# Four operand splits and one softmax scaling moved between engines in the attention stage of a hybrid trunk kernel

## The chip, the cores and the metric

The kernel runs on one NeuronCore of a Trainium2 chip, in one launch. The metric is the device time of that launch in microseconds. The kernel before took 1543.39 us (median of three runs, 1543.29 to 1546.81). The engines are called as the profile calls them: PE (matrix products and transposes), DVE (VectorE), ACT (ScalarE), POOL (GpSimd) and SP (the queue that issues most DMAs). Each engine works through its instructions in order.

## The reference

One layer over 1024 frames of width 1024, in 32-bit floats. The parts that matter here, cut short:

```python
def band_attention(q, k, v, qn_g, kn_g, rel_bias):      # 8 heads of 64, chunks of 64 frames
    qh = head_rms(q, qn_g); kh = head_rms(k, kn_g)
    scores = einsum('bnqhd,bnkhd->bnhqk', qc, kb) * 64 ** -0.5   # own chunk and the 8 before
    scores = where(valid, scores + bias, -1e30)
    probs = softmax(scores, axis=-1)
    o = einsum('bnhqk,bnkhd->bnqhd', probs, vb)

h = rmsnorm(x, norm_mix_g)
oa = hgrn2_mixer(...)                                   # 4 heads of 128, a gated recurrence
ob = band_attention(...)
merged = sigmoid(gate_a) * (oa @ w_branch_a) + sigmoid(gate_b) * (ob @ w_branch_b)
x = x + merged @ w_out
x = x + (silu(h2 @ w_gate) * (h2 @ w_up)) @ w_down      # h2 = rmsnorm(x)
x = x + sigmoid(h3 @ w_ple_gate) * (p @ w_ple_proj)     # h3 = rmsnorm(x)
```

## The kernel before

**Split operands.** A large product keeps nearly full precision by taking each operand as two: `hi` is the value rounded to the PE's fast type (a cast, on ACT), `lo` is the remainder, value minus `hi` (a subtraction). Three products, hi·hi, hi·lo and lo·hi, are summed in PSUM (`gemm`). Weights come as 128x1024 pieces: a load into `wr`, a cast to `wh` on ACT (L142) and a remainder `wl`, in the attention stage on GpSimd (L149, L150). Activations lie in `s` tiles ("slots").

**Stages.** The projections and norms come first, then the four heads of the recurrence, woven with projections for the attention; then the attention itself; then `branches`, which multiplies `oa` and `ob` with the branch weights; then the output product, the feed-forward part and the last gate. Between the recurrence and the branches the four tiles of `oa` lie in DRAM.

**The attention stage** (`attention`, L721) runs 32 steps. Step n takes a pair of heads and a block of 128 queries: steps 0 to 15 take the blocks of pairs 0 and 1 in turn, steps 16 to 31 those of pairs 2 and 3. Work of neighbouring steps overlaps. Step n, in the order that the code records it:

- head 1 of step n-1 gets its reciprocal and scaling (`stage(n - 1, 1)`);
- a piece of other PE work (`next(feed)`): up to step 27 the projections of the later pairs of queries and keys, from step 29 on the branches;
- the scores of step n, and on DVE the sum with the bias and the running extreme, straight from PSUM (a custom operation);
- in odd steps the products of probabilities and values for steps n-3 and n-2;
- `stack(n + 1)`: two transposes of the next queries and keys, two ACT copies out of PSUM that round them, and two DVE remainders; then another piece of feed;
- the transposes of head 1 of step n-1 (`pt(n - 1, 1)`), the exponentials of both heads of step n on ACT, the transposes of head 0 of step n-1 (`pt(n - 1, 0)`), then head 0's reciprocal on DVE and scaling.

The profile names head 0's scores `m` and head 1's `s`; their transposes are `pm<-eye,m` and `pm<-eye,s` at L105. A step with all five blocks in its band has 128x640 scores per head; the first blocks of a pair have 128, 256, 384 and 512.

**What sets the order.** Operations called through `self.V`, `self.A`, `self.G`, `self.load`, `self.mul` and `self.tr` are pinned: each engine executes them in the order in which the Python code calls them (the helper at L72, for DMAs L97, for matmuls L102, for transposes L105). Operations called on the engine directly, the weight casts of L142 among them, are placed by the scheduler. GpSimd's instructions in this stage are all pinned: powers for the norms of queries and keys (`m<-m,mhalf`, in odd steps), the weight remainders `wl` and the issues of accumulating DMAs (`next(self.adds)`, odd steps, and in `branches`).

**The branch operands.** `branch_load` loads the four `oa` tiles back (`raws`), and at the end of four steps, listed in `SPLITS`, one of them is split: a pinned ACT cast and a pinned DVE remainder. The pairs are read by the branch products, the first of them in step 29 (the first two) and step 30 (the last two).

Of the kernel before, what the change touches and what calls it, by code (L numbers as in the profile page):

```python
# [11 lines left out]
F32R = mybir.dt.float32r  # L12
U8 = mybir.dt.uint8
U32 = mybir.dt.uint32
AF = mybir.ActivationFunctionType
ALU = mybir.AluOpType
# [6 lines left out]
HALF = 512  # L23
NFF = 22
STEPS = (NFF // 2 + 1) // 2
SPLITS = (24, 26, 27, 28)
EPS = 1e-6
LEVELS = (1, 2, 4, 8, 16)
TURN = 32
# [15 lines left out]
def f32(ap):  # L45
    return ap.bitcast(F32)
# [28 lines left out]
class Trunk:  # L75
# [585 lines left out]
    def attn_scores(self, pair, b):  # L661

        nb = min(b + 1, 5)
        cols = nb * P
        k0 = (b + 1 - nb) * P
        na = {1: 1, 2: 2, 3: 3, 4: 2, 5: 3}[nb] * P
        q1, q2 = self.qs.pop((pair, b))
        k1, k2 = self.ks[pair % 2]
        parts = [(lo, hi) for lo, hi in ((0, na), (na, cols)) if hi > lo]
        banks = [[self.mm() for _ in parts] for _ in range(2)]  # L670
        for i, (lo, hi) in enumerate(parts):
            c = slice(k0 + lo, k0 + hi)
            for j, (q, k) in enumerate(((q1, k1), (q1, k2), (q2, k1))):
                for h in range(2):
                    r = slice(64 * h, 64 * h + 64)
                    self.mul(banks[h][i][:, :hi - lo], q[r, :], k[r, c], start=j == 0, stop=j == 2)

        def softmax(h):
            bias = self.bias[pair, h]
            s = self.slot(late=True)[:, :640] if h else self.small(640, tag="s")  # L680
            mx = self.small(2, tag="mx2")
            last = None
            for i, (lo, hi) in enumerate(parts):
                init = 3.0e38 if last is None else last
                self.V.tensor_tensor_reduce(
                    s[:, lo:hi], banks[h][i][:, :hi - lo], bias[:, 640 - cols + lo:640 - cols + hi], -1.0, init, ALU.add, ALU.min, mx[:, i:i + 1])
                last = mx[:, i:i + 1]
            yield s, nb
            den = self.small(1, tag="den")
            self.A.activation(s[:, :cols], s[:, :cols], AF.Exp, bias=last, scale=-1.0, accum_out=den)  # L690
            yield
            self.V.reciprocal(den, den)
            if h == 0:
                self.A.activation(s[:, :cols], s[:, :cols], AF.Copy, scale=den)
            else:
                self.V.tensor_scalar(s[:, :cols], s[:, :cols], den, None, ALU.mult)

        return [softmax(h) for h in range(2)]

    def attn_pt(self, s, nb):  # L700
# [20 lines left out]
    def attention(self):  # L721

        steps = [(2 * two + p, b) for two in range(2) for b in range(8) for p in range(2)]
        whole = len(steps)
        feed = self.feed
        sc, pts = {}, {}

        def stack(n):
            if n >= whole:
                return iter(())  # L730
            p, b = steps[n]
            if b == 0:
                for h in range(2):
                    bt = self.small(640, tag="bias")
                    self.load(bt, self.d["bias"][2 * p + h])
                    self.bias[p, h] = bt
            return self.attn_stack(p, b)

        def scores(n):
            for h, stages in enumerate(self.attn_scores(*steps[n])):  # L740
                sc[n, h] = (*next(stages), stages)

        def stage(n, h):
            if 0 <= n < whole:
                next(sc[n, h][2], None)

        def pt(n, h):
            if 0 <= n < whole:
                pts[n, h] = self.attn_pt(*sc[n, h][:2])

        def pv(n):
            if 0 <= n < whole:
                self.attn_pv(*steps[n], (pts.pop((n, 0)), pts.pop((n, 1))), sc[n, 0][1])

        for i in range(FIRST, 8):
            next(feed, None)
            if i == FIRST:
                self.hgrn_gate()
            if i == 7:
                drain(stack(0))  # L760
                drain(self.hgrn_out())
        drain(self.copies)
        self.adds = chain(self.osum, self.wsum)
        for n in range(whole + 2):
            if n % 2 and n < whole:
                next(self.adds)
            stage(n - 1, 1)
            next(feed, None)
            if n < whole:
                if steps[n][1] == 0:  # L770
                    self.ob.append(self.slot())
                scores(n)
            if n % 2:
                pv(n - 3)
                pv(n - 2)
            drain(stack(n + 1))
            if n < whole - 3 or n >= whole:
                next(feed, None)
            pt(n - 1, 1)
            stage(n, 0)  # L780
            stage(n, 1)
            pt(n - 1, 0)
            stage(n, 0)
            self.rest(False)
            if n > whole - 5:
                self.rest(False)
            if n == 0:
                self.keep_heads(self.oa, self.od, self.done_heads)
            if n == whole // 2 + 3:
                self.keep_heads(self.ob, self.obd, [0, 1])  # L790
            if n == whole - 10:
                raws = self.branch_load(self.od)
            if n in SPLITS:
                raw = raws[len(self.osrc)]
                hi, lo = self.slot(F32R), self.slot(F32R)
                self.A.copy(hi, raw)
                self.V.tensor_tensor(lo, raw, f32(hi[:, :]), ALU.subtract)
                self.osrc.append((hi, lo))
            if n == whole - 4:
                while self.queue:  # L800
                    self.rest()
                self.queue = None
                self.gate_load()
                self.gate_load()
                self.branch = self.branches()
                feed = chain(feed, self.branch)
            yield 0
        self.keep_heads(self.ob, self.obd, [2, 3])
# [1283 lines left out]
def drain(stream):  # L2092
    while True:
        try:
            next(stream)
        except StopIteration as e:
            return e.value
# [125 lines left out]
```

## Time and profile before

| | us |
|---|---|
| median of three runs | 1543.39 |
| the runs | 1546.81, 1543.29, 1543.39 |
| the profiled execution | 1546.48 |
| its span | 1544.7 |
| PE, DVE, ACT, GpSimd busy | 1517.0, 1107.8, 661.5, 634.2 |
| attention stage, about | 448 to 646 of the span |

A row of a timeline gives start and duration in us, engine, line of the code, operation, output and inputs by the program's names, partitions x elements, count, and in brackets the time that the engine sat idle before it and what ended that wait. A row of a windows table gives a stretch of the span, its length, then the busy time and count of instructions of PE, PE's weight loads, DVE, ACT and GpSimd, then the clock granted to the PE (1.00 is full speed), the DMA engines' share and GB/s. In tables of waits, "X <- Y: a, b, c" means that X waited for Y a us in total, in b waits, the longest c. The chain of waits is the work that ended last, followed back.

### The profile page before, as it was taken

To read this page: it belongs to the slowest core of one execution; us is meant where nothing else is said; L and a number is where in the kernel's file an instruction comes from. 1 tells how busy PE (TensorE), PEld (TensorE's weight loads), DVE (VectorE), ACT (ScalarE), POOL (GpSimd) and SP (SyncE) were. 2 spreads that over 40 slices of the span, in tenths; PEclk is the share of its full clock that TensorE was granted. 3 is DMA by queue.
4 is the path that set the end of the run, shared out by engine and by line. 5 is a ranking of instruction groups with operands and counts; after the bars stand their busy time and mean duration, and the time that the engine had idled before them with its cause. 6 is when DMAs were issued, how large, how long until landed. Compare 5 with 4: busy or idle time off the path is not lost.

```text
span 1544.7 us, 20689 instructions
## 1 busy us (share of the span) xinstructions
PE 1517.0 (98%) x7692; PEld 1252.4 (81%) x7692; DVE 1107.8 (72%) x1603; ACT 661.5 (43%) x1109; POOL 634.2 (41%) x353
## 2 busy tenths in 40 slices
PE   8999999999999998999999999999999999999998
PEld 6888888888877877788888888888888888888886
DVE  5777776577766767547888877777777757756678
ACT  6633333433346767522566222222222234456452
POOL 4233333101132423245212656665555545545546
PEclk9999999999999999999999999999999999999999
DMA  5552434698543365476346244443333288775335
GB/s 207 190 170 82 143 144 148 222 323 304 183 137 64 93 168 157 142 220 224 118 145 214 99 117 126 124 128 114 106 102 103 102 308 319 275 271 179 127 101 199
DMA packets 97908, 258.66 MB, mean 167 GB/s; under 512 B 10128, under 2 KB 14992, under 8 KB 97296
## 3 DMA queue, kind: packets, MB, share of 16 engines
q1 hardware_dynamic: 91264, 241.60, 44.8%
q0 software_dynamic: 6400, 15.73, 6.1%
q8 instruction: 60, 0.98, 0.2%
q14 instruction: 40, 0.33, 0.1%
q10 hardware_dynamic: 144, 0.02, 0.0%
HBM read 194.13 MB, written 94.63 MB: 187 GB/s over the span
## 4 chain that ended last, share of the span: by engine, by line
PE 91%; DVE 5%; DMA 1%; ACT 1%; issue 1%; SPq 0%; POOL 0%; DVEq 0%; ACTq 0%; POOLq 0%
PE pm L102 89%; DVE s L72 3%; PE pm L105 3%; DMA m<-d 0%; ACT wh L142 0%; DMA s<-in_x 0%; DVE m L72 0%; ACT s L72 0%; DMA wr<-in_fm 0%; ACT m L72 0%; DMA wr<-in_wv 0%; DVE s L337 0%; SPq L97 0%; DVE s L234 0%; DVE wl L72 0%
## 5 line engine op out<-in xcount | busy, mean ns | idle before, releaser
L102 PE MATMUL pm<-s,whi 128*128 128x512 f32 x1848 | 568.9, 389 | 0.0
L102 PE MATMUL pm<-s,wh 128*128 128x512 f32 (+1 forms) x1520 | 472.2, 392 | 6.8 <-ACT wh L142 5.2
L102 PEld LDWEIGHTS pm<-s,whi 128*128 128x128 f32 x1848 | 346.8, 188 | 72.0 <-DVE t L72 0.2
L102 PE MATMUL pm<-s,wlo 128*128 128x512 f32 x924 | 359.4, 389 | 0.0
L102 PEld LDWEIGHTS pm<-s,wh 128*128 128x128 f32 x1520 | 284.5, 189 | 66.6 <-ACT wh L142 5.2
L72 DVE TENSOR_TENSOR s<-s,s 128x512 f32<-128x512 f32 (+3 forms) x240 | 293.3, 1251 | 60.7 <-ACT s L72 47.0
L102 PE MATMUL pm<-s,wl 128*128 128x512 f32 (+1 forms) x760 | 296.4, 390 | 0.5 <-POOL wl L150 0.5
L150 POOL TENSOR_TENSOR wl<-wr,wh 128x1024 fp32r<-128x1024 f32 (+2 forms) x72 | 175.7, 2445 | 220.8 <-ACT wh L142 209.8
L72 DVE TENSOR_TENSOR t<-pm,t 128x512 f32<-128x512 f32 x163 | 112.2, 689 | 140.9 <-PE pm L102 118.4
L102 PEld LDWEIGHTS pm<-s,wlo 128*128 128x128 f32 x924 | 173.5, 188 | 36.0
L142 ACT CAST wh<-wr 128x1024 fp32r<-128x1024 f32 (+2 forms) x104 | 104.2, 1005 | 206.9 <-PE pm L102 90.0
L102 PE MATMUL pm<-wh,s 128*128 128x512 f32 x512 | 181.9, 409 | 0.0
L102 PEld LDWEIGHTS pm<-s,wl 128*128 128x128 f32 x760 | 143.3, 189 | 31.0 <-POOL wl L150 1.2
L72 POOL TENSOR_TENSOR wlo<-q,whi 128x512 fp32r<-128x512 f32 x64 | 102.6, 1604 | 151.9 <-ACT whi L72 81.6
L72 POOL TENSOR_TENSOR wlo<-wr,whi 128x1024 fp32r<-128x1024 f32 (+1 forms) x65 | 136.0, 2099 | 68.0 <-ACT whi L72 58.9
L72 POOL TENSOR_TENSOR m<-m,mhalf 128x8 f32<-128x8 f32 (+1 forms) x24 | 35.1, 1462 | 223.4 <-DVE m L72 223.4
L72 ACT CAST whi<-q 128x512 fp32r<-128x512 f32 (+1 forms) x96 | 72.8, 758 | 106.9 <-PE pm L102 87.1
L72 ACT CAST s<-s 128x1024 fp32r<-128x1024 f32 (+1 forms) x98 | 94.4, 982 | 55.2 <-DVE s L72 32.0
L102 PEld LDWEIGHTS pm<-wh,s 128*128 128x128 f32 x512 | 97.0, 189 | 18.9 <-DVE m L72 0.2
L72 POOL TENSOR_TENSOR s<-t,rb 128x512 f32<-128x512 f32 x44 | 71.2, 1619 | 99.4 <-ACT t L72 99.4
L102 PE MATMUL pm<-wl,s 128*128 128x512 f32 x256 | 100.5, 393 | 0.0
L72 ACT ACTIVATE t<-s 128x512 f32<-128x512 f32 x44 | 27.8, 633 | 158.6 <-DVE s L72 154.5
(151 smaller groups left out, 1758.5 us busy)
## 6 DMA issues: line engine op xcount, KB each, us to landing
s<-d SPq DMA_DIRECT2D x83, 512.0 KB, 6.2
d<-s SPq DMA_DIRECT2D x87, 256.0 KB, 2.3
wr<-d SPq DMA_DIRECT2D x36, 512.0 KB, 3.5
d<-s SPq DMA_DIRECT2D x32, 512.0 KB, 4.3
d<-t SPq DMA_DIRECT2D x50, 256.0 KB, 2.6
wr<-in_sz SPq DMA_DIRECT2D x22, 512.0 KB, 5.8
wr<-in_sg SPq DMA_DIRECT2D x22, 512.0 KB, 3.7
wr<-in_su SPq DMA_DIRECT2D x22, 512.0 KB, 4.1
```

Source lines behind the costliest of these rows:

```text
L72: return lambda *a, **k: self.trunk.order(op(*a, **k), self.key)
L102: return self.order(self.nc.tensor.matmul(*a, **k))
L105: return self.order(self.nc.tensor.transpose(*a, **k))
L142: self.nc.scalar.copy(hi[:, c], raw[:, c])
L150: rest.tensor_tensor(lo[:, c], raw[:, c], f32(hi[:, c]), ALU.subtract)
```

## The change

Three things change, all in the attention stage:

1. The scaling of head 0's probabilities, 32 instructions of up to 128x640, goes from ACT to GpSimd, pinned there. Head 1's stays on DVE.
2. Each of the four splits of branch operands moves from the end of a step to the place behind `stack(n + 1)`, in front of the second piece of feed, and its remainder goes from DVE to GpSimd. The steps are 23, 25, 27 and 28 in place of 24, 26, 27 and 28.
3. The loads of the four operands are recorded one step earlier (step 21 in place of 22).

```diff
-SPLITS = (24, 26, 27, 28)
+SPLITS = (23, 25, 27, 28)
...
             self.V.reciprocal(den, den)
-            if h == 0:
-                self.A.activation(s[:, :cols], s[:, :cols], AF.Copy, scale=den)
-            else:
-                self.V.tensor_scalar(s[:, :cols], s[:, :cols], den, None, ALU.mult)
+            (self.V if h else self.G).tensor_scalar(s[:, :cols], s[:, :cols], den, None, ALU.mult)
...
             drain(stack(n + 1))
+            if n in SPLITS:
+                raw = raws[len(self.osrc)]
+                hi, lo = self.slot(F32R), self.slot(F32R)
+                self.A.copy(hi, raw)
+                self.G.tensor_tensor(lo, raw, f32(hi[:, :]), ALU.subtract)
+                self.osrc.append((hi, lo))
             if n < whole - 3 or n >= whole:
                 next(feed, None)
...
-            if n == whole - 10:
+            if n == whole - 11:
                 raws = self.branch_load(self.od)
-            if n in SPLITS:
-                raw = raws[len(self.osrc)]
-                hi, lo = self.slot(F32R), self.slot(F32R)
-                self.A.copy(hi, raw)
-                self.V.tensor_tensor(lo, raw, f32(hi[:, :]), ALU.subtract)
-                self.osrc.append((hi, lo))
```

The order of GpSimd's instructions at the end of the stage, from step 27 on, as the difference of the two programs. `m_6143` and `m_6147` are the power of step 27; `s_6136` and `s_6214` remainders of branch operands; `m_6095`, `m_6197`, `m_6294`, `m_6386`, `m_6454` head 0 of steps 27 to 31; `wl` remainders of branch weights:

```order
-L72 TENSOR_TENSOR m_6143<-m_6143,mhalf 128x8
+L72 TENSOR_TENSOR s_6136<-s_5639,s_6135 128x1024
+L72 TENSOR_TENSOR m_6147<-m_6147,mhalf 128x8
+L72 TENSOR_SCALAR m_6095<-m_6095,m_6161 128x640
+L72 TENSOR_TENSOR s_6214<-s_5641,s_6213 128x1024
+L72 TENSOR_SCALAR m_6197<-m_6197,m_6227 128x640
 L72 DMA d_3019<-d_2971 128x1024
 L72 TENSOR_TENSOR wl_6254<-wr_6256,wh_6255 128x1024
 L72 TENSOR_TENSOR wl_6260<-wr_6262,wh_6261 128x1024
 L72 DMA d_3170<-d_3119 128x1024
+L72 TENSOR_SCALAR m_6294<-m_6294,m_6344 128x640
+L72 TENSOR_SCALAR m_6386<-m_6386,m_6412 128x640
```

The scaling of step 29 (`m_6294`) now stands behind the two weight remainders and a DMA issue; before, GpSimd had no softmax work at all.

ACT in step 29 and at the start of step 30, before: the exponentials of step 29 (`m_6294`, `s_6298`), head 0's scaling, two copies of the stack, two copies of transposes (`m_6348`, `m_6402`), and the casts of the two branch weights.

```order
L72 ACTIVATE m_6294,m_6344<-m_6294,m_6295 128x640
L72 ACTIVATE s_6298,m_6346<-s_6298,m_6299 128x640
L72 COPY m_6348<-pm_6349 128x384
L72 ACTIVATE m_6294<-m_6294,m_6344 128x640
L72 ACTIVATE s_3912<-pm_6394,cols 128x128
L72 ACTIVATE m_6397<-pm_6394,ones 128x128
L72 COPY m_6402<-pm_6403 128x384
L142 CAST wh_6255<-wr_6256 128x1024
L142 CAST wh_6261<-wr_6262 128x1024
```

And with the change:

```order
L72 ACTIVATE m_6294,m_6344<-m_6294,m_6295 128x640
L72 ACTIVATE s_6298,m_6346<-s_6298,m_6299 128x640
L72 COPY m_6348<-pm_6349 128x384
L142 CAST wh_6255<-wr_6256 128x1024
L72 ACTIVATE s_3912<-pm_6394,cols 128x128
L72 ACTIVATE m_6397<-pm_6394,ones 128x128
L142 CAST wh_6261<-wr_6262 128x1024
L72 COPY m_6402<-pm_6403 128x384
```

The scaling is gone, and the first cast stands where it stood; both casts are still behind the exponentials of step 29.

DVE at the end of step 27 and the start of step 28, before (copies of transposes out of PSUM, the reciprocals, the remainder `s_6174`, head 1's scaling, and a scaling of queries and keys):

```order
L72 COPY m_6147<-pm_6153 128x256
L72 COPY m_6161<-pm_6167 128x256
L72 RECIPROCAL m_6157<-m_6157 128x1
L72 TENSOR_TENSOR s_6174<-s_5706,s_6173 128x1024
L72 RECIPROCAL m_6159<-m_6159 128x1
L72 TENSOR_SCALAR s_6099<-s_6099,m_6159 128x640
L72 TENSOR_TENSOR m_6179<-pm_5981,m_6143 128x512
```

And with the change:

```order
L72 COPY m_6151<-pm_6157 128x256
L72 COPY m_6165<-pm_6171 128x256
L72 RECIPROCAL m_6161<-m_6161 128x1
L72 RECIPROCAL m_6163<-m_6163 128x1
L72 TENSOR_SCALAR s_6099<-s_6099,m_6163 128x640
L72 TENSOR_TENSOR m_6179<-pm_5985,m_6147 128x512
```

The remainder between the two reciprocals is gone; the rest keeps its order.

## The prediction

> **What bounds the kernel now.** I read the page's first part, then the PE's waits inside the attention stage, then the chain of waits, and only then single rows of the four engines.
>
> ```profile
> PE 1517.0 (98%) x7692; PEld 1252.4 (81%) x7692; DVE 1107.8 (72%) x1603; ACT 661.5 (43%) x1109; POOL 634.2 (41%) x353
> ...
> PE 91%; DVE 5%; DMA 1%; ACT 1%; issue 1%; SPq 0%; POOL 0%; DVEq 0%; ACTq 0%; POOLq 0%
> ```
>
> The matrix engine is busy for 98% of the span and carries 91% of the chain. Work taken off the other engines is worth something only where the PE waits for it. The change touches the attention stage alone, from about 448 to 646 us of the span. The PE's waits there, in us in total, times and longest, are these:
>
> ```profile
> PE pm L105 <- DVE s L72: 4.4, 2, 3.8
> PE pm L102 <- DVE m L72: 1.2, 1, 1.2
> PE pm L105 <- ACT m L72: 0.8, 2, 0.5
> PE pm L105 <- DVE m L72: 0.4, 1, 0.4
> ```
>
> That is 6.8 us in all, and 3.8 of it is one stall. The chain of waits shows what leads up to that stall (start, us, what):
>
> ```profile
> 611.08 0.83 DVE m L72 x3
> ...
> 611.93 0.83 ACT m L72
> 612.76 0.94 ACT s L72
> ...
> 613.73 1.23 DVE s L72
> ...
> 615.06 0.56 DVE s L72
> ...
> 615.76 2.37 PE pm L105 x10
> ```
>
> This is step 27 turning into step 28. DVE finishes copying transposes and takes head 0's reciprocal. ACT then scales head 0 (611.93) and makes the cast of a branch operand (612.76). DVE, in order, waits for that cast, does the 1.23 us remainder, and only then scales head 1 (615.06), for which the PE's transposes wait. So a cast and a remainder that nothing needs for another 2 us or more stand in front of work that the PE needs at once. The rows of the PE around it (start, us):
>
> ```profile
> 615.76 1.30 PE L105 MATMUL pm<-eye,s 128*128 128x128 f32 x5 [3.78 <-DVE s L72]
> 616.86 1.27 PE L105 MATMUL pm<-eye,m 128*128 128x128 f32 x5
> 617.78 1.12 PE L102 MATMUL pm<-s,wh 128*128 128x512 f32 x2
> ...
> 627.69 0.74 PE L105 MATMUL pm<-eye,s 128*128 128x128 f32 x5
> 628.94 0.77 PE L105 MATMUL pm<-eye,m 128*128 128x128 f32 x5 [0.51 <-ACT m L72]
> 629.47 0.70 PE L102 MATMUL pm<-s,wh 128*128 128x512 f32 x2
> ...
> 635.15 0.82 PE L105 MATMUL pm<-eye,s 128*128 128x128 f32 x5 [0.64 <-DVE s L72]
> 636.26 0.73 PE L105 MATMUL pm<-eye,m 128*128 128x128 f32 x5 [0.29 <-ACT m L72]
> ```
>
> After the stall the same three groups take 1.30, 1.27 and 1.12 us where they later take 0.74, 0.77 and 0.70: 1.5 us more. The granted clock (the third last column of the windows) says why:
>
> ```profile
> 616.00:618.00 2.00, 2.00 (x11) 2.00 (x11) 1.71 (x8) 1.12 (x2) 0.00 (x0) 0.50 0.71 137
> ```
>
> **The change, part by part.** *Loads one step earlier: 0.* The four loads stand at the same place of SP's queue in both programs, and SP is far ahead of the steps: they go out as the four `s<-d` here, some 30 us before the first cast.
>
> ```profile
> 552.61 2.41 SPq L97 DMA_DIRECT2D s<-d  x4
> ```
>
> *Remainders and casts.* Four remainders of 1.23 us leave DVE and become four GpSimd ones. GpSimd does this shape (two inputs, 128x1024) in 2.38 us, and 128x512 in 1.29 us:
>
> ```profile
> 513.05 2.38 POOL L72 TENSOR_TENSOR wl<-wr,wh 128x1024 fp32r<-128x1024 f32 x1 [1.42 <-ACT wh L142]
> ...
> 119.96 1.29 POOL L72 TENSOR_TENSOR wlo<-q,whi 128x512 fp32r<-128x512 f32 x1 [6.10 <-ACT whi L72]
> ```
>
> The cast comes behind the stack's two copies, in step 27 behind this one, so it runs from about 607.3 to 608.4 and the remainder to 610.8, before the power that GpSimd owes in that step starts (611.32):
>
> ```profile
> 607.04 0.36 ACT L72 ACTIVATE m<-pm,ones 128x128 fp32r<-128x128 f32 x1
> ...
> 611.32 1.66 POOL L72 TENSOR_TENSOR m<-m,mhalf 128x8 f32<-128x8 f32 x1 [6.24 <-DVE m L72]
> ```
>
> DVE is then free of the wait. Its reciprocals at 611.74 follow each other, 0.15 us each, and head 1's scaling (0.55) ends near 612.65. The PE starts 0.15 us later, as it did at 615.76 behind 615.06 + 0.56: at 612.8.
>
> *Head 0's scaling.* Thirty-two instructions of up to 128x640 leave ACT for GpSimd; the trace has no GpSimd operation with one tensor input. Upper bound: the line through the two rows above gives 0.2 + 640 x 2.13 ns = 1.57 us for two inputs. Lower bound: DVE's 0.55 us for the same operation and shape. I take 1.2, nearer the GpSimd rows and below them because one input is read instead of two. In step 27 it waits for the power's end: 612.98 + 1.2 + 0.15 = 614.3 for head 0's transposes, which now start at 616.86. **Gain 2.5 us**, and the slow clock behind it, (1.27 - 0.77) + (1.12 - 0.70) = **0.9 us**, goes too.
>
> *What is queued in front of it.* GpSimd works in order, and in step 29 the order puts two weight remainders and a DMA issue ahead of head 0's scaling (the first order fence above). Before, they were nobody's hurry:
>
> ```profile
> 629.92 4.73 POOL L72 TENSOR_TENSOR wl<-wr,wh 128x1024 fp32r<-128x1024 f32 x2 [16.10 <-ACT wh L142]
> 634.60 0.79 POOL L72 DMA_DIRECT2D d<-d  x1
> ```
>
> They had waited 16.1 us for their casts, which ACT keeps behind its exponentials of step 29:
>
> ```profile
> 626.51 0.46 ACT L72 COPY m<-pm 128x384 f32<-128x384 f32 x1
> 626.93 0.83 ACT L72 ACTIVATE m<-m,m 128x640 f32<-128x640 f32 x1
> ...
> 628.16 0.36 ACT L72 ACTIVATE m<-pm,ones 128x128 fp32r<-128x128 f32 x1
> 628.41 0.48 ACT L72 COPY m<-pm 128x384 f32<-128x384 f32 x1
> 628.77 2.01 ACT L142 CAST wh<-wr 128x1024 fp32r<-128x1024 f32 x2
> ```
>
> In the changed order the first cast takes the place of the scaling at 626.93 (the second order fence above), the second comes behind the two copies. On the clock of before: first cast done 627.98, remainder from 628.1 to 630.45, the second to 632.8, the DMA issue to 633.6, the scaling to 634.8, and the PE's transposes of head 0 at 634.95. They follow head 1's directly and would be ready at 628.43, and started at 628.94. No PE work stands between, so this is a stall of 6.5 us and **a loss of 6.0 us** against before. Steps 29 and 30 have moved forward together by then, ACT and GpSimd through DVE and the PE, so the distance stays. A stall longer than the one at 615.76 should bring its slow clock back: **1.5 us lost** (bounds 0 and 1.5). The stalls of 0.64 and 0.29 us in step 31 go, since DVE and ACT are ahead there: **gain 0.9 us**.
>
> *The early steps.* In even steps nothing stands ahead of the scaling, and its transposes come in the next step. In odd ones it follows a power; at step 15:
>
> ```profile
> 543.60 1.69 POOL L72 TENSOR_TENSOR m<-m,mhalf 128x8 f32<-128x8 f32 x1 [10.44 <-DVE m L72]
> ...
> 546.94 0.71 PE L105 MATMUL pm<-eye,m 128*128 128x128 f32 x5
> ```
>
> 545.29 + 1.2 + 0.15 = 546.64, 0.3 us to spare, and about 0.1 us late at 1.57. I count 0. ACT's 32 lost scalings are worth 0 themselves: ACT waits for PE or DVE in every one of these steps, and the PE's 0.8 us on ACT is in the terms above.
>
> *The sum:* -2.5 - 0.9 + 6.0 + 1.5 - 0.9 = **+3.2 us**. The profiled execution took 1546.48 us (span 1544.7 and 1.8 around it) and would take 1549.7; it lies 3.1 above the median, so on the median of 1543.39 the forecast is **1546.6 us**. With 0.55 us for the scaling it is 1.3 less (it counts in steps 27 and 29), with 1.57 us 0.7 more; without the slow clock 1.5 less. Its own range is 1543.5 to 1548.5.
>
> **The rivals.** *A, faster: the queue does not bite.* If the two weight remainders ran when their data came, the loss of 6.0 and its clock would vanish, the 0.51 us at 628.94 too: -2.5 - 0.9 - 0.5 - 0.9 = -4.8, 1538.6 us. For it: they had 16.1 us of idle GpSimd in front. Against: that idle time was ACT's order, which still has the casts behind the exponentials. Chance 0.10.
>
> *B, slower: GpSimd is slower at this than its two-input rows.* It decides from 1.5 us on, where the 0.3 us to spare at step 15 is spent. At 2.4 us each of the five odd steps of full width ahead of step 27 (9, 11, 13, 15, 25) is some 0.9 us late (545.29 + 2.4 + 0.15 - 546.94), 4.5 in all, and steps 27 and 29 add 1.2 each: +3.2 + 6.9 = +10.1, 1553.5 us. Against it, only that one input should not cost more than two. Chance 0.14.
>
> *C, slower: the two engines exclude each other in every odd step.* DVE's scaling suffers when GpSimd streams, but not when GpSimd is in a power:
>
> ```profile
> 632.64 2.36 DVE L72 TENSOR_SCALAR s<-s,m 128x640 f32<-128x640 f32 x1
> ...
> 518.60 1.66 POOL L72 TENSOR_TENSOR m<-m,mhalf 128x8 f32<-128x8 f32 x1 [0.17 <-DVE m L72]
> ...
> 519.28 0.55 DVE L72 TENSOR_SCALAR s<-s,m 128x640 f32<-128x640 f32 x1
> ```
>
> The first, 2.36 instead of 0.55 us, ended 0.35 us behind the weight remainders above (629.92 + 4.73); the last ran whole inside the power (518.60 to 520.26). If the power did exclude it, and GpSimd went straight on to its scaling, head 1 in step 15 would end at 545.29 + 1.2 + 0.35 = 546.84, and its transposes, 0.54 us before 546.94, would be 0.6 us late; in five such steps 3.0, so +6.2, 1549.6 us. In even steps the wait is real, but the next step's products with the values stand ahead of the transposes on the PE and cover it. Chance 0.06.
>
> The Trainium skill, "SBUF — State Buffer", section "SBUF: two separate sides", states rival C's rule: the port pair that the two engines share is locked for a whole instruction by whichever starts first. By that rule the time is C's 1549.6; the trace agrees for the streaming remainder and not for the power (0.55 us inside one), so it gets the small chance.
>
> **How the numbers follow.** Forecast 0.66, A 0.10, B 0.14, C 0.06, anything else 0.04. About 0.3%, 4.6 us, is what can be told from no change, so faster means under 1538.8 and slower over 1548.0. Most of A is faster: 0.08. B, C and the upper end of the forecast's own range are slower: 0.28. The rest, 0.64, is no change. The range that should hold 8 in 10 leaves out most of A and B: 1541.5 to 1550.5 us.
>
> **What would show it.** In the new profile the 3.8 us wait of the PE for DVE's `s` should be gone, and a single wait of 5 to 7 us for a GpSimd `m` should stand near 625 us, with a granted clock near 0.5 right after it. GpSimd's `TENSOR_SCALAR` 128x640 should take between 0.55 and 1.57 us, and no other wait for it should pass 0.3 us. The forecast is wrong if the two weight remainders run before the exponentials of step 29 (then A), or if the PE waits for GpSimd in many odd steps (then B or C, told apart by the duration of the GpSimd scaling and of DVE's).

## The result, and the profile after

The changed kernel took **1554.7 us** (median of five runs, 1552.36 to 1559.28), the kernel before, run beside it, 1545.05 (1543.29 to 1546.81). The ratio is 1.0066, 95% interval 1.0055 to 1.0077: slower by 0.55 to 0.77%. The forecast was 1546.6, 3.2 us slower and so most likely no change, with a range to 1550.5. Measured were some 10 us, so both the verdict and the size were missed; rival B's 1553.5 is the nearest number. The profiled execution took 1552.82 us, its span is 1550.7. The first and the fourth part of its page (busy time, chain of waits):

```profile
PE 1517.8 (98%) x7692; PEld 1252.8 (81%) x7692; DVE 1108.0 (71%) x1599; ACT 642.5 (41%) x1077; POOL 691.4 (45%) x389
...
PE 88%; DVE 5%; issue 2%; DMA 2%; POOL 2%; ACT 1%; SPq 0%; POOLq 0%; DVEq 0%; ACTq 0%
```

19 us of work left ACT (661.5 before), and 57 us more stand on GpSimd (634.2 before). GpSimd, at 0% of the chain before, now has 2%. The PE's waits inside its attention stage:

```profile
PE pm L105 <- POOL m L72: 9.5, 5, 7.0
PE pm L102 <- DVE m L72: 1.8, 1, 1.8
PE pm L105 <- DVE m L72: 1.0, 1, 1.0
PE pm L105 <- DVE s L72: 0.7, 1, 0.7
```

The stall of 3.8 us behind DVE's `s` is gone, and in its place the PE waits 9.5 us for GpSimd's `m`, head 0's probabilities, 7.0 of it at once.

**Where the time went, by thirds of the stage.** The PE runs its products in the same order in both kernels, so the same row can be found in both traces. Three marks cut the stage: the first transposes of step 0's head 1, the scores of step 28, and the transposes of step 28's head 0; a branch product behind the transposes of step 31 ends it. Rows of the PE's timeline, before:

```profile
460.12 0.28 PE L105 MATMUL pm<-eye,s 128*128 128x128 f32 x1
...
609.30 1.86 PE L102 MATMUL pm<-s,m 64*128 64x384 f32 x12
...
624.22 0.80 PE L105 MATMUL pm<-eye,m 128*128 128x128 f32 x5
...
644.50 0.72 PE L102 MATMUL pm<-s,wh 128*128 128x512 f32 x2
```

And after:

```profile
457.14 0.28 PE L105 MATMUL pm<-eye,s 128*128 128x128 f32 x1
...
609.52 1.14 PE L102 MATMUL pm<-s,m 64*128 64x384 f32 x12
...
622.88 0.71 PE L105 MATMUL pm<-eye,m 128*128 128x128 f32 x5
...
650.51 0.72 PE L102 MATMUL pm<-s,wh 128*128 128x512 f32 x2
```

Between the marks lie 149.18, 14.92 and 20.28 us before, 152.38, 13.36 and 27.63 after. The change costs **+3.20 us in the early steps, -1.56 where step 27 turns into 28, and +7.35 in steps 29 to 31**, 8.99 in all. The prediction's terms for these thirds were 0, -3.4 and +6.6. The first mark itself lies 3 us earlier after than before; it lies between 455.8 and 457.6 in all twelve kernels other than the one before, so it was that one profiled execution that was late ahead of the stage, where the code of all kernels is the same. The experiments are read by the same marks.

| kernel | ratio to before (95%) | early | 27/28 | 29 to 31 | stage |
|---|---|---|---|---|---|
| the whole change | 1.0066 (1.0055 to 1.0077) | +3.20 | -1.56 | +7.35 | +8.99 |
| 1: scaling alone | 1.0067 (1.0053 to 1.0081) | +3.25 | -1.56 | +9.49 | +11.18 |
| 2: splits alone | 0.9965 (0.9951 to 0.9978) | +0.08 | -2.52 | -0.69 | -3.13 |
| 3: steps 29 to 31 on ACT | 1.0009 (0.9998 to 1.0020) | +3.27 | -1.64 | -0.24 | +1.39 |
| 4: odd steps on ACT too | 0.9971 (0.9960 to 0.9982) | -0.03 | -2.62 | -0.72 | -3.37 |
| 5: as 2, remainder on DVE | 0.9960 (0.9948 to 0.9972) | -1.12 | -4.07 | -0.09 | -5.28 |
| 6: remainder on GpSimd, old place | 0.9958 (0.9946 to 0.9970) | -0.60 | -4.76 | 0.00 | -5.36 |
| 7: two-input scaling | 1.0027 (1.0017 to 1.0038) | -0.59 | -2.30 | +7.26 | +4.37 |
| 8: as 2, even steps | 0.9962 (0.9950 to 0.9975) | -0.64 | -4.77 | -0.70 | -6.11 |
| 9: as 7, steps 29 to 31 on ACT | 0.9969 (0.9957 to 0.9980) | -0.50 | -2.32 | -0.27 | -3.09 |
| 11: as 8, step 29's head 0 on DVE | 0.9950 (0.9937 to 0.9962) | -0.61 | -4.78 | -1.33 | -6.72 |

The last four columns are one profiled execution each, in us against before. They follow the timed ratios within 2.5 us.

**The end of the stage.** The PE's timeline around its long wait, in the changed kernel:

```profile
626.26 0.71 PE L105 MATMUL pm<-eye,s 128*128 128x128 f32 x5
633.96 1.33 PE L105 MATMUL pm<-eye,m 128*128 128x128 f32 x5 [7.00 <-POOL m L72]
```

The window behind that wait, with the granted clock at 0.50 (third last column):

```profile
634.00:636.00 2.00, 2.00 (x8) 1.81 (x9) 0.64 (x4) 0.48 (x1) 0.00 (x0) 0.50 0.90 178
```

GpSimd's timeline ahead of it:

```profile
626.57 4.68 POOL L72 TENSOR_TENSOR wl<-wr,wh 128x1024 fp32r<-128x1024 f32 x2 [6.07 <-ACT wh L142]
631.16 0.81 POOL L72 DMA_DIRECT2D d<-d  x1
631.75 2.15 POOL L72 TENSOR_SCALAR m<-m,m 128x640 f32<-128x640 f32 x1
```

This is the predicted queue, row for row: GpSimd idles 6.07 us until ACT's first weight cast is done, does both weight remainders and the DMA issue, and only then the scaling for which the PE stands still.

**The early steps.** The costliest GpSimd group in the stage is the new one (16 of the 32, the rest are smaller shapes; busy us, mean ns):

```profile
L72 POOL TENSOR_SCALAR m<-m,m 128x640 f32<-128x640 f32 x16 | 31.5, 1972 | 15.3 <-DVE m L72 15.1
```

1.97 us in the mean and 1.88 where nothing disturbs it, where the prediction took 1.2 and held 1.57 for the upper bound. In odd steps it follows a power, and the PE waits (timeline, step 11):

```profile
516.63 1.67 POOL L72 TENSOR_TENSOR m<-m,mhalf 128x8 f32<-128x8 f32 x1
518.31 1.88 POOL L72 TENSOR_SCALAR m<-m,m 128x640 f32<-128x640 f32 x1
...
520.25 0.77 PE L105 MATMUL pm<-eye,m 128*128 128x128 f32 x5 [0.39 <-POOL m L72]
```

Against before, head 0's transposes lose 0.26, 0.56, 0.21, 0.17, 0.48 and 0.55 us in this way (steps 1, 11, 15, 17, 23, 25): 2.23 of the 3.20. Another 0.65 is lost at step 12, which the last section comes to.

### The profile page after: what moved, and what is told of

The parts are those of the page before. It is cut to its first block, busy times and chain, and to the rows that moved or that the text cites. A ratio compares the mean times of both kernels' runs of the same rounds, so it can differ in the third digit from the quotient of the medians.

```text
span 1550.7 us, 20764 instructions
## 1 busy us (share of the span) xinstructions
PE 1517.8 (98%) x7692; PEld 1252.8 (81%) x7692; DVE 1108.0 (71%) x1599; ACT 642.5 (41%) x1077; POOL 691.4 (45%) x389
## 4 chain that ended last, share of the span: by engine, by line
PE 88%; DVE 5%; issue 2%; DMA 2%; POOL 2%; ACT 1%; SPq 0%; POOLq 0%; DVEq 0%; ACTq 0%
PE pm L102 86%; DVE s L72 3%; PE pm L105 2%; POOL m L72 1%; DMA wr<-in_wv 1%; DVE m L72 1%; POOL wl L72 1%; ACT s L72 0%; ACT m L72 0%; DMA wr<-in_fm 0%; DMA s<-in_x 0%; ACT wh L142 0%; DMA wr<-in_qk 0%; DVE s L234 0%; SPq L97 0%
## 5 line engine op out<-in xcount | busy, mean ns | idle before, releaser
L72 DVE TENSOR_TENSOR s<-s,s 128x512 f32<-128x512 f32 (+3 forms) x236 | 288.0, 1249 | 57.0 <-ACT s L72 43.4
```

The lines of the kernel that those rows point to most:

```text
L72: return lambda *a, **k: self.trunk.order(op(*a, **k), self.key)
```

## The experiments

The theory after the result had two parts: the one-input scaling is dear on GpSimd and late in every odd step, and the queue of step 29 costs what was predicted. The rival was that the moved splits cost, or that GpSimd hinders DVE wherever it works.

### Each half alone

**1, the scaling alone:** the kernel before, with only this line.

```diff
-            if h == 0:
-                self.A.activation(s[:, :cols], s[:, :cols], AF.Copy, scale=den)
-            else:
-                self.V.tensor_scalar(s[:, :cols], s[:, :cols], den, None, ALU.mult)
+            (self.V if h else self.G).tensor_scalar(s[:, :cols], s[:, :cols], den, None, ALU.mult)
```

> The kernel before with one part of the change: head 0's 32 scalings on GpSimd; the four splits and the loads stay where they were. Theory (the scaling on GpSimd, queued there behind other work, is what costs): the PE waits for GpSimd's head 0 in the odd steps (about 3.3 us up to step 26) and once for 6 to 7 us in step 29/30, with 1.5 us of slow clock behind it, while the DVE stall of 3.8 us in step 27 stays or shrinks to about 2; that is 8 to 11 us over the kernel before, 1553 to 1556, no better than the whole change. Rival (the moved splits cost, the scaling is cheap): within 4 us of the kernel before, 1545 to 1549, and no single wait over 2 us for a GpSimd m.

Measured: 1555.66 us against 1545.15, as slow as the whole change, with nearly the same sum in the early steps, +3.25 us. That the sums agree is partly chance: only 1.0 us of it is lost at head 0's transposes, 0.64 more goes into the wait at step 12 (1.83 us), and 1.6 is lost behind that wait, where the clock is granted at 0.50 from 518 to 521 us. The changed kernel waits 1.84 us at the same place and keeps its clock at 1.00. Two of the PE's waits in its stage:

```profile
PE pm L105 <- POOL m L72: 9.1, 2, 8.9
PE pm L105 <- DVE s L72: 2.5, 1, 2.5
```

**2, the splits alone:** the changed kernel with head 0's scaling back on ACT (the diff above, reversed).

> The other part alone: the splits and loads as in the changed kernel, head 0's scaling back on ACT. Theory: the 3.8 us stall of step 27 and its 1.5 us of slow clock go, and nothing replaces them: 4 to 6 us under the kernel before, about 1540. Rival (the remainders on GpSimd hold DVE up, since a DVE scaling of 128x8 took 1.27 to 1.30 us beside them in the changed kernel's trace): at most 3 us under the kernel before, 1542 to 1545, with PE waits for DVE of 1 us or more in steps 23, 25, 27 and 28.

Measured: 1539.7 us against 1545.15. The loss is all the scaling's; the splits gain. The rival was right in a smaller matter: the PE waits around step 27 for DVE, 0.96, 0.71 and 0.35 us. Experiments 5, 6 and 8 take that up.

### The queue of step 29, and the odd steps

**3** puts the scalings of steps 29 to 31 back on ACT, **4** those of all odd steps too; the rest is the changed kernel. The edit of 3; in 4 the condition is `h == 0 and (pair % 2 or 16 * (pair // 2) + 2 * b > 28)`, since a step is odd where its pair is.

```diff
-            (self.V if h else self.G).tensor_scalar(s[:, :cols], s[:, :cols], den, None, ALU.mult)
+            if h == 0 and 16 * (pair // 2) + 2 * b + pair % 2 > 28:
+                self.A.activation(s[:, :cols], s[:, :cols], AF.Copy, scale=den)
+            else:
+                (self.V if h else self.G).tensor_scalar(s[:, :cols], s[:, :cols], den, None, ALU.mult)
```

> The changed kernel with the scalings of steps 29, 30 and 31 alone back on ACT; 29 of the 32 stay on GpSimd. Theory (the queue of two weight remainders and a DMA issue in step 29 is most of the loss): the wait of 7.0 us goes, and most of the slow clock of 2.2 us behind it: 7 to 9 us under the changed kernel, 1546 to 1548, 1 to 3 over the kernel before. Rival (duration: every odd step pays, and the wait in step 29 would only move to the next late thing): at most 4 us under the changed kernel, 1550 or more.

> As the kernel with steps 29 to 31 on ACT, and the scalings of all odd steps on ACT too; GpSimd keeps the 15 of the even steps 0 to 28. Theory (a scaling of 1.9 to 2.2 us on GpSimd is late only where it stands behind a power, that is in odd steps): the losses of steps 1, 11, 15, 17, 23 and 25 (2.2 us together), the 1.4 us wait in step 27 and its clock go: 3 to 5 us under the kernel with 29 scalings, 1542 to 1544, and 1 to 3 under the kernel before. Rival (GpSimd's streaming holds DVE up wherever it runs): no better than that kernel by more than 1 us, with waits of the PE for DVE in even steps.

Measured: 1545.96 and 1540.43 us against 1545.15; the second is a larger gain than its theory's 1542 to 1544. Three instructions out of 32 are worth 7.6 us of the stage (+7.35 to -0.24), and the early +3.27 stays as it was; with the odd steps on ACT it is -0.03. So the two losses are separate, and 15 scalings in even steps cost nothing. They gain nothing either: 4 and 2 agree (1540.43 and 1539.7, stage -3.37 and -3.13), so relieving ACT of them is worth nothing that these runs can tell.

### What makes the scaling dear

**7** is the whole change with the same product in the two-input form; order and number of instructions are unchanged.

```diff
-            (self.V if h else self.G).tensor_scalar(s[:, :cols], s[:, :cols], den, None, ALU.mult)
+            if h:
+                self.V.tensor_scalar(s[:, :cols], s[:, :cols], den, None, ALU.mult)
+            else:
+                self.G.tensor_tensor(s[:, :cols], s[:, :cols], den.to_broadcast([P, cols]), ALU.mult)
```

> The whole change, with GpSimd's scaling written as an operation with two tensor inputs (probabilities, and the reciprocal repeated along the row) instead of one tensor and a number per row; the order of all engines is unchanged. Theory (duration counts in odd steps, and the one-input form is the dearer one: 1.88 to 2.2 us measured against 0.2 + 640 x 2.13 ns = 1.57 us by the rows of the remainders): 1.6 us each, the PE's waits for GpSimd in odd steps (0.39, 0.32, 0.40 and 1.44 us) go or shrink by 0.3 each, the one of 7.0 by 0.3 to 0.5: 1.5 to 3 us under the whole change, 1551.5 to 1553. Rival (GpSimd's cost is per element and row whatever the form): 1.9 us or more each, and within 1 us of the whole change.

Measured: 1548.47 us against 1544.33, more of a gain than the theory's 1551.5 to 1553. The group of the scaling in its stage:

```profile
L72 POOL TENSOR_TENSOR m<-m,m 128x640 f32<-128x640 f32 x16 | 21.1, 1318 | 19.4 <-DVE m L72 19.4
```

And its timeline with the queue of step 29 and the stall:

```profile
622.11 4.67 POOL L72 TENSOR_TENSOR wl<-wr,wh 128x1024 fp32r<-128x1024 f32 x2 [6.38 <-ACT wh L142]
626.71 0.81 POOL L72 DMA_DIRECT2D d<-d  x1
627.27 1.51 POOL L72 TENSOR_TENSOR m<-m,m 128x640 f32<-128x640 f32 x1
...
628.84 1.33 PE L105 MATMUL pm<-eye,m 128*128 128x128 f32 x5 [6.31 <-POOL m L72]
```

1.32 instead of 1.97 us, and the whole early loss is gone (+3.20 to -0.59), while the end stays (+7.26). The theory had put the two-input form at 1.57 us by the line through the remainders; this one is cheaper than that line.

**10** replaces the reciprocal of each row by a constant, to ask whether the number per row is what costs. It leaves out head 0's division by its sum; only the duration was asked for.

```diff
-            (self.V if h else self.G).tensor_scalar(s[:, :cols], s[:, :cols], den, None, ALU.mult)
+            (self.V if h else self.G).tensor_scalar(s[:, :cols], s[:, :cols], den if h else 0.01, None, ALU.mult)
```

> The whole change with GpSimd's one-input scaling by a constant, 0.01, in place of each row's reciprocal: this leaves out head 0's division by its sum, so its time is that of a smaller computation. Only the duration of the GpSimd operation of 128x640 is asked for. If the number per row is what makes the one-input form dear, it takes under 1.4 us (the two-input form took 1.32); if the one-input form is dear as such, 1.8 to 2.0 as with the number per row.

The group of the scaling in its stage:

```profile
L72 POOL TENSOR_SCALAR m<-m 128x640 f32<-128x640 f32 x16 | 31.1, 1961 | 13.4 <-ACT m L72 13.4
```

1.96 us, and 1.81 where nothing disturbs it (1.88 with the number per row): the one-input form is dear as such, and its number per row adds 0.07 us.

**9** puts both remedies together, the two-input form and steps 29 to 31 on ACT.

> The whole change with GpSimd's scaling in the two-input form (4.1 us over the kernel before, 1.32 us each) and the scalings of steps 29 to 31 on ACT. Theory (two causes make the whole loss: the one-input form's 1.88 to 2.2 us in odd steps, and the queue of step 29): with both gone the wait of 6.3 us and its clock go, 6 to 8 us under the two-input kernel, 2 to 4 under the kernel before, 1540.5 to 1542.5, with the wait of 0.77 us for GpSimd in step 27 left over. Rival (something else of the GpSimd scaling still costs, say DVE's operations held up beside it): 1543 or more, with PE waits for DVE above those of the kernel with the moved splits alone.

Measured: 1541.3 us against 1545.68. Early -0.50, end -0.27, the stage -3.09; with all the scalings on ACT, in 2, it is -3.13. Nothing of the loss is left in the sum, so the two causes account for it, as far as one profiled execution of each kernel can tell. The 29 scalings cost nothing on GpSimd in this form and bring nothing; the wait of 0.77 us for GpSimd in step 27 is left over, as expected.

### What the splits gain, and through what

**5** is 2 with the four remainders on DVE at the new place (first lines); **6** is the kernel before with the four remainders on GpSimd at the old place (last lines).

```diff
-                self.G.tensor_tensor(lo, raw, f32(hi[:, :]), ALU.subtract)
+                self.V.tensor_tensor(lo, raw, f32(hi[:, :]), ALU.subtract)
...
-                self.V.tensor_tensor(lo, raw, f32(hi[:, :]), ALU.subtract)
+                self.G.tensor_tensor(lo, raw, f32(hi[:, :]), ALU.subtract)
```

> As the kernel with the moved splits alone (1539.7), but the four remainders stay on DVE at the new place, behind the stack's copies. Theory (the place is what counts: at the new place the cast comes before the exponentials, so DVE's wait for it is over long before head 1's scaling is due): the 3.8 us stall of step 27 is gone here too, within 2 us of that kernel, 1538 to 1541. Rival (the engine is what counts: 1.23 us of remainder and the wait for the cast now stand ahead of DVE's part of the power and of its copies): waits of the PE for DVE in steps 23, 25, 27 and 28 grow by 1 us or more each in at least two of them, 1542 to 1545.

> The kernel before with the four remainders on GpSimd, nothing else: casts, steps and place as before. Theory (either the engine or the place suffices, since the stall was DVE's in-order wait for a cast nobody needed yet): the 3.8 us stall shrinks to under 1 and its slow clock goes, 3.5 to 5.5 us under the kernel before, 1539.5 to 1541.5. Rival (the place is needed, the cast still stands behind head 0's scaling on ACT and pushes the next step's exponentials): under 2 us of gain, 1543 or more.

Measured: 1538.47 and 1538.2 us against 1544.33, the second below its theory's 1539.5 to 1541.5. Either move alone ends the 3.8 us stall; 0.70 and 1.02 us of that wait are left, the second just over its theory's 1 us. Their timed ratios can't be told from 2's, but in the trace both do better than the two moves together: -4.07 and -4.76 us in 27/28 against -2.52. One row that differs is DVE's 128x8 operation ahead of the power. In the timeline of 2 it is 1.28 us long, beside GpSimd's remainder at the new place:

```profile
606.15 2.37 POOL L72 TENSOR_TENSOR s<-s,s 128x1024 fp32r<-128x1024 f32 x1 [2.61 <-issue]
...
607.27 1.28 DVE L72 TENSOR_SCALAR m<-m,m 128x8 f32<-128x8 f32 x1
```

In that of 6 it takes 0.23 us, and GpSimd has nothing running then:

```profile
606.10 0.23 DVE L72 TENSOR_SCALAR m<-m,m 128x8 f32<-128x8 f32 x1
```

The larger part of the difference comes with the clock. From 612 to 614 us it is granted at 0.50 in 2, and in 5, 6 and 8 it stays at 1.00 through the whole turn of step 27. The same products of the branches right behind head 0's transposes, in the PE's timeline of 2 and of 6:

```profile
612.19 1.22 PE L102 MATMUL pm<-s,wh 128*128 128x512 f32 x2
...
610.06 0.73 PE L102 MATMUL pm<-s,wh 128*128 128x512 f32 x2 [0.20 <-DVE m L72]
```

The PE's waits there add up to 2.02 us in 2, 1.25 in 6 and 1.88 in 5, where DVE does the remainder itself just ahead. So the hold-up of the 128x8 operation can explain some 0.8 of 6's 2.24 us and little of 5's 1.55. Why the clock held in 5, with waits nearly as long as in 2, is open.

**8** keeps 2's place and engine and changes only the steps, to the even ones, which have no power.

```diff
-SPLITS = (23, 25, 27, 28)
+SPLITS = (22, 24, 26, 28)
```

> As the kernel with the moved splits alone (1539.7), but in steps 22, 24, 26 and 28, the even ones, in which neither GpSimd nor DVE has a power to do. Theory (what is left of the stalls in step 27, 0.96 + 0.71 + 0.35 us, is DVE's 128x8 operation of the power held up to 1.28 us by the remainder beside it): those three waits fall to 0.5 together, 1 to 2 us under that kernel, 1537.5 to 1539. Rival (the hold-up moves with the remainder, to the DVE scaling of the even steps, 0.55 us when alone): within 0.7 us of that kernel, with new waits of the PE for DVE in steps 22, 24 or 26.

Measured: 1537.55 us against 1544.33, -4.77 us in 27/28, level with 6; the waits there are 1.03 and 0.20 us, more than the theory's 0.5 in all, and no new wait for DVE stands in steps 22, 24 or 26, as the rival had it. By time alone 8 and 2 can't be told apart (0.9950 to 0.9975, 0.9951 to 0.9978).

**11** adds to 8 that head 0 of step 29 is scaled on DVE. ACT's unpinned weight cast had taken its place ahead of the copies there, in 2, 4 and 8, and the PE waited 1.18 us for them in 2 and 8, 1.16 in 4.

```diff
-            if h == 0:
+            if h == 0 and 16 * (pair // 2) + 2 * b + pair % 2 != 29:
```

> As the kernel with the splits in steps 22, 24, 26 and 28 (1537.6), with head 0's scaling of step 29 on DVE. There the PE waited 1.18 us for ACT's copies, which stand behind the scaling (0.85) and a weight cast (1.05). Theory (ACT's order at that place sets it): the wait falls to 0.4 or less and the kernel is 0.5 to 1 us faster, 1536.5 to 1537. Rival (DVE's scaling beside the remainders of weights on GpSimd takes over 1 us and holds the next scores' sums): no gain, 1537.5 or more.

The wait in the PE's timeline:

```profile
619.91 0.76 PE L105 MATMUL pm<-eye,m 128*128 128x128 f32 x5 [0.54 <-ACT m L72]
```

The wait falls to 0.54 us, not to the 0.4 of the theory, and the stage is 0.61 shorter than 8's in the trace; the times (1538.83 against 1545.68) can't tell that from nothing. With a ratio of 0.9950 (0.9937 to 0.9962) this version beats the kernel before by 0.4 to 0.6%; the whole change's ratio, 1.0066, lies 1.2% above it.

## Why the prediction was wrong, point by point

**The early steps, counted 0, measured +3.20: the step that failed.** It hung on the duration of the scaling: 1.2 us taken, "upper bound" 1.57 from GpSimd's two-input rows, on the argument that one input should not cost more than two. It measured 1.88 us undisturbed and 1.97 in the mean, so the bound was none. Head 0's transposes, late in six odd steps, lose 2.23 of the 3.20 us; 0.65 is the wait at step 12, and some 0.3 is spread over small differences. At 1.2 the sum said 0.3 us to spare in step 15; at 1.88 it says 545.29 + 1.88 + 0.15 - 546.94 = 0.38 late, and 0.21 was measured. The prediction had this as rival B, decision point included (1.5 us), and gave it 0.14 on the same argument. B's price was too high per step (0.9 us, from 2.4 us each) and it counted five steps where six were late.

**With that number put right, the sum nearly holds: experiment 7.** There the scaling takes 1.32 us, close to the 1.2 assumed, and the kernel comes out 4.1 us slower than before (by the ratio's interval 2.6 to 5.9), where +3.2 was forecast. That it comes so near is partly luck: its thirds are -0.59, -2.30 and +7.26 us where 0, -3.4 and +6.6 were forecast, so the middle term is wrong there too. In the change itself 3.2 of the 5.8 us by which the stage misses the forecast are early, 1.8 in the middle and 0.75 at the end.

**Remainders and casts: right.** Head 1's transposes of step 27 were to start at 612.8 on the clock of before. The times can be set side by side, since step 28's scores start at 609.30 before and 609.52 after; that they do is chance, 3 us less ahead of the stage and 3.2 more in it. The changed kernel's timelines have both heads' transposes, and head 0's scaling:

```profile
612.79 0.74 PE L105 MATMUL pm<-eye,s 128*128 128x128 f32 x5 [0.70 <-DVE s L72]
614.97 1.32 PE L105 MATMUL pm<-eye,m 128*128 128x128 f32 x5 [1.44 <-POOL m L72]
...
613.03 1.89 POOL L72 TENSOR_SCALAR m<-m,m 128x640 f32<-128x640 f32 x1
```

That DVE would be held up beside GpSimd's remainder was not in the working. It shows as 0.98 us of waiting for DVE's `m` just ahead (0.39 before). Experiments 6 and 8 show that about 2.2 us more were to be had in 27/28, some 0.8 in waits and the rest in the clock.

**Head 0's scaling in step 27: -2.5 and -0.9, mis-sized.** Its transposes were to start at 614.3 and start at 614.97, 0.67 later, as 1.88 us in place of 1.2 makes them. The slow clock comes back behind it (the group of five takes 1.32 us, not 0.77), so the 0.9 is lost too. That the 1.44 us wait is what brings it is not shown: in 2 and 4, where no wait for GpSimd stands there, the clock falls to 0.50 at the same place. So the step "the slow clock goes with the stall" failed too. The middle column measured -1.56 where -3.4 was forecast, and -2.30 with the two-input form.

**The queue of step 29: +6.0, right.** The transposes lose 6.45 us against before, 7.00 of wait against a forecast 6.5. Rival A (the remainders run when their data come, and the queue does not bite) is excluded by the 6.07 us that GpSimd idles for ACT's cast ahead of them. **The slow clock behind it: +1.5, measured 2.2** (0.45, 1.28 and 0.50 us in the three groups behind the stall): the bound at 1.5 was taken from a shorter stall. **The stalls of step 31: -0.9, measured -1.2.** Together +6.6 forecast, +7.35 measured; 3 shows that the three scalings are the cause.

**Rival C (the engines exclude each other in every odd step): not by the power.** In the changed kernel's timeline DVE's scaling of step 11 ran in 0.56 us inside GpSimd's power (516.63 + 1.67):

```profile
517.37 0.56 DVE L72 TENSOR_SCALAR s<-s,m 128x640 f32<-128x640 f32 x1
```

**The way from trace to median: right.** Subtracting 3.1 us for the profiled execution of before is borne out by the first mark: that execution was some 3 us late before the stage began. The median itself was less firm: over five runs it is 1545.05, 1.7 us higher than over three.

## What to carry to other kernels

Before moving an operation to another engine, find a row of that very form on that engine; where none exists, the rows of a neighbouring form bound nothing, and the range has to say so. An engine with idle time is not free at the moment that counts: what stands in its queue ahead of the moved work, and what that waits for, sets the price, and three instructions out of 32 cost most of the loss here. Where two edits cure one stall, run each alone: here each did at least as well as both together.

## What the runs showed of the hardware

**GpSimd's one-input form costs more than its two-input form.** For 128x640 it takes 1.88 us undisturbed (1.97 in the mean) with a number per row and 1.81 (1.96) with a constant, and 1.24 (1.32) as a product of two tensors of which one repeats along the row. The Trainium skill, "GPSIMD Engine Reference", section "4.1 Engine selection", has it the other way round: about half VectorE's pace for two inputs, and roughly line rate for one. The traces agree for two inputs (the 128x1024 remainder takes 2.38 us on GpSimd and 1.23 on DVE) and not for one: DVE scales 128x640 in 0.55 us, GpSimd in 3.4 times that. Why, no run here shows.

**GpSimd's remainders hold up even a tiny DVE operation.** DVE's 128x8 operation takes 0.23 us alone and 1.24 to 1.54 beside a weight remainder, ending as the remainder ends. At step 12 of the changed kernel, where the two weight remainders run back to back, it cost the PE 1.84 us of waiting (1.18 before, 1.43 in 2 without a scaling on GpSimd, 0.75 with the two-input form). The changed kernel's timeline:

```profile
511.52 5.00 POOL L72 TENSOR_TENSOR wl<-wr,wh 128x1024 fp32r<-128x1024 f32 x2
...
515.01 1.54 DVE L72 TENSOR_SCALAR m<-m,m 128x8 f32<-128x8 f32 x1
...
516.93 0.61 PE L102 MATMUL pm<-s,m 64*128 64x256 f32 x5 [1.84 <-DVE m L72]
```

511.52 + 5.00 = 516.52 and 515.01 + 1.54 = 516.55. The wait is as long (1.83 us) in 1 and 3, the other kernels of the table with the one-input scaling in odd steps. So a dearer operation can cost twice, in its own queue and through what it pushes into a collision, though 2's 1.43 says that not all of the wait is its doing.

**The one-input scaling holds DVE up only at its start.** DVE's scaling of 128x640 takes 0.55 us alone. In the changed kernel's timeline it ran at full pace inside GpSimd's, 0.65 us behind its start:

```profile
644.02 1.88 POOL L72 TENSOR_SCALAR m<-m,m 128x640 f32<-128x640 f32 x1 [4.75 <-DVE m L72]
...
644.67 0.56 DVE L72 TENSOR_SCALAR s<-s,m 128x640 f32<-128x640 f32 x1
```

Where it began 0.25 to 0.39 us behind, it took 0.76 to 0.89, each time ending 1.14 us after GpSimd's start. In 7, where it began 0.26 to 0.70 us behind the two-input scaling, it took 0.90 to 1.35 us, each time ending 0.35 us behind GpSimd's operation. The other way round, GpSimd's one-input scaling takes 2.21 and 2.23 us where DVE's began just ahead of it; 2.15 was also measured with no DVE operation beside it, behind a DMA issue.

The Trainium skill, "SBUF — State Buffer", section "SBUF: two separate sides", states a rule of this kind, an exclusive lock on a port pair that DVE and GpSimd share, held for the whole instruction. The rows of the remainders and of 7's scaling agree with it. The power and the one-input scaling do not: DVE's scaling ran inside each of them in 0.56 us.
